# A gated mixer projected token-major: v's input as the stationary operand, its weights moving, in two passes over the weights

## The chip, the cores and the metric

One core of a Trainium2 chip runs the kernel. The metric is device time in microseconds (us), the median of several executions of one program. One more execution was taken with the profiler on; the rows below come from that one.

## The reference, cut to what matters

One layer of a hybrid decoder works on 2048 prompt tokens and on 8 samples of one token each, D_MODEL = 1024, everything in float32:

```
h = rms_norm(x) * (1 + scale(c)) + shift(c)                 # adaLN
p = h @ w_in        # columns: q k v (3*512) | z 512 | beta alpha | u 512 | vb 512
# head group A: gated DeltaNet, 4 heads of 128, chunks of 64, with a running state
# head group B: spatial gating
vn = rms_norm_per_head(gelu(vb)) * w                        # per token and head, over 128
v2 = w_sgu[h] (128x128, lower triangular) applied over the tokens of a 128-chunk + b
mixB = gelu(u) * v2
x1 = x + gate * ([mixA, mixB] @ w_out)
y  = x1 + gate2 * ConvFFN(adaLN(x1))
# each sample also updates its own states S (4 heads x 128 x 128):  S <- eg*S + k v^T
```

Two facts matter here. The sgu of head group B normalizes vb over the 128 channels of a head, and then mixes over tokens. And each sample has a state of 128x512 numbers that is read, updated and written back.

## The kernel before, in words

**Precision.** A float32 operand is split into a high and a low part (`split`: ACT copies the high part, L100, and DVE subtracts for the low one, L97). A product is three matmuls: high by high, high weights by low input, low weights by high input (`gemm_steps`, L113 to L115). Ordinarily the weights are the stationary operand (128x128) and the input hh, hl, channel-major, is the moving one, so that results stand with channels on the partitions and tokens along the free axis.

**Stages.** The mixer runs over four segments of 512 prompt tokens. Segment 0 also carries the samples' 8 columns: 520 columns, in blocks of 2x260. A segment does q, k and v of the delta group (`qkv_tile`, with the 16 squarings and solves of the chunks between), then the sgu's four heads (`sgu`, and `sgu_post` one head behind), then the z tiles woven with the delta chain (`scan`), then the out projection (`out_proj`, with the next segment's first stage between its tiles). The FFN follows, in three column blocks.

**Weights.** A block of weights is 128x512 in two parts, 512 KB (`wblock`). In segment 0 it comes raw through SP's queue (`wslab`, L147, tile wr, 128x1024 and so two blocks), is split on ACT and DVE, used, and stored in DRAM, also through SP's queue (L160, `kept_*`). From segment 1 on POOL's queue reads the stored 512 KB back (L156, `w<-kept_w_in`). Raw and split tiles share one ring of six (tag "w").

**PSUM.** Products use three banks (tag g), transposes and small results two (tag t), the chain's results two (tag c).

**Order.** A scheduler arranges each engine's instructions within what the tiles allow. Each engine, and each engine's DMA queue, runs its instructions strictly in the order that results: an instruction that waits holds back everything behind it. On SP that means that a store that waits for its data holds the loads behind it.

**The sgu before.** `sgu(h)` projects v (act_tile(20 + h)) and u (act_tile(16 + h)) with channels on the partitions. `sgu_post` transposes v back to token rows on PE (four 128x128 transposes, L653), sums squares on ACT (L424), takes root and reciprocal (L657, L658), scales on DVE (L660, four), applies the 128x128 token mixing on PE (L664), and multiplies by u on POOL.

**The delta chain's inversion.** `solve_merge` writes the solved blocks to DRAM (`td<-sv`, L508) and reads them back in another layout (`lt<-td`, L511) into one of three tiles with tag lt. DVE rearranges them, and PE multiplies (L525).

**The samples' states.** `smp_state` runs between the out projection's tiles of segment 0. For each of eight samples a 256 KB state is loaded (L759, tile cv), DVE makes a masked key (L847, km), PE makes the outer products (L849), DVE combines (L851, four), and SP stores the state (L853). The states go through tiles with tag cv. There are four, and the masked values vm hold one.

Of the kernel before, what the change touches and what calls it, by code (L numbers as in the profile page):

```python
# [45 lines left out]
def trunk(ctx, tc, A, O):  # L46
# [98 lines left out]
    def wslab(src):  # L145
        raw = wp.tile([128, 1024], F32, tag="w", name="wr", bufs=6)
        nc.sync.dma_start(out=raw, in_=src)  # L147
        return raw
# [152 lines left out]
    def cv_slabs():  # L301
        while True:
            yield cv()[:, 0:512]
# [333 lines left out]
    def act_tile(*a):  # L637
        run(act_steps(*a))

    def sgu(h, hx, W, extra):  # L640
        uv = uvt()
        act_tile(20 + h, hx, W, AF.Gelu_apprx_tanh, uv[:, 0, 0:SEG], gvs[:, h, :])
        next(extra, None)
        act_tile(16 + h, hx, W, AF.Gelu_apprx_tanh, uv[:, 1, 0:SEG], us[:, h, :])
        next(extra, None)
        return uv

    def sgu_post(h, uv, W, mix):
        off = W - SEG
        v, u = uv[:, 0, 0:SEG], uv[:, 1, 0:SEG]  # L650
        tp = pst()
        for t in range(4):
            PE.transpose(tp[:, t * 128:(t + 1) * 128], v[:, t * 128:(t + 1) * 128], ident)  # L653
        ss = small((128, 4), "sgs")
        for t in range(4):
            square_sum(tp[:, t * 128:(t + 1) * 128], ss[:, t:t + 1], "v")
        S_.activation(out=ss, in_=ss, func=AF.Sqrt, scale=1.0 / 128, bias=epst[:, 0:1])  # L657
        V.reciprocal(out=ss, in_=ss)  # L658
        for t in range(4):
            V.tensor_scalar(out=v[:, t * 128:(t + 1) * 128], in0=tp[:, t * 128:(t + 1) * 128],  # L660
                            scalar1=ss[:, t:t + 1], scalar2=None, op0=ALU.mult)
        ps = pst()
        for t in range(4):
            PE.matmul(ps[:, t * 128:(t + 1) * 128], v[:, t * 128:(t + 1) * 128], wsT[:, h, :], start=True, stop=True)  # L664
# [161 lines left out]
    def smp_state(sk, vn, eg):  # L826
# [13 lines left out]
        vm = cv()[0:32, 0:512].rearrange("p (h v) -> p h v", h=4)  # L840
# [3 lines left out]
        for b in range(NS):  # L844
            s0 = load_state(b, cv()[:, 0:512])
# [341 lines left out]
    for s in range(NSEG):  # L1187
# [34 lines left out]
        extra = mod_half(4, cv_slabs()) if s == 0 else iter(())  # L1222
        for hd in range(4):
            uv = sgu(hd, h, W, extra)
            if hd:
                sgu_post(hd - 1, pend, W, mix)
            else:
                v_head(3, vf[3], Z)
                solve_merge(Z)
# [6 lines left out]
        sgu_post(3, pend, W, mix)  # L1236
# [120 lines left out]
def _layout(i):  # L1357
# [19 lines left out]
        "w_in": tiles(cols), "w_ba": w_in[:, 2048:2056].reshape(8, 128, 8).transpose(1, 0, 2),  # L1377
# [43 lines left out]
```

## Time and profile before

| | us |
|---|---|
| median of 3 runs | 2552.92 (2552.12 to 2553.29) |
| profiled execution | 2546.75 |
| span of its records | 2545.0 |
| PE busy, share of the span | 2422.3, 95% |
| DVE busy | 1701.6, 67% |
| ACT busy | 1040.6, 41% |
| POOL busy | 631.6, 25% |

The profiled execution lies 6.2 us under the median of the runs without a profile, and 1.75 us of it lie outside the span. A change that is worked out from rows moves the span, and is then added to the median. A busy time counts the time in which an instruction of the engine runs. A busy PE can still run at half its clock, which a row of the windows shows as a granted clock of 0.50.

### The profile page before, as it was taken

Reading aid. Unit: us, or ns where it says so; the run is one execution under the profiler, and the core shown is the slowest. Engines: PE = TensorE matmul, PEld = TensorE weight load, DVE = VectorE, ACT = ScalarE, POOL = GpSimd, SP = SyncE. Lnnn points to the kernel's source line nnn. Section 1 sums busy time; section 2 is a strip of 40 time slices with the busy share of each in tenths; the row PEclk is TensorE's granted clock in tenths of the full one; section 3 lists DMA queues with packets and bytes.
Section 4 is the critical chain, followed back from the end, with each engine's and each line's share of the span. In section 5 each row is a group of like instructions: output and inputs, shape, how many; then the busy total and the mean of one; then the engine's idle time right before and its main releaser. Section 6 shows DMA issues by size and latency. Waiting matters only on the chain.

```text
span 2545.0 us, 41928 instructions
## 1 busy us (share of the span) xinstructions
PE 2422.3 (95%) x15770; PEld 2241.5 (88%) x15770; DVE 1701.6 (67%) x3603; ACT 1040.6 (41%) x2137; POOL 631.6 (25%) x897
## 2 busy tenths in 40 slices
PE   7889989999999999989999998899999898999997
PEld 4788967888888878889999998899999898999997
DVE  4676667454735563799999998665556685665565
ACT  5756635465445634454444444322222242211213
POOL 0110003211311221311111115433333353333333
PEclk9999989999999999999999999999999999999998
DMA  9775777566746664898777778877777668776773
GB/s 370 243 255 173 255 230 252 158 194 195 203 129 211 213 172 135 288 330 310 289 296 288 296 284 294 265 244 231 230 225 228 218 211 265 232 230 219 229 233 118
DMA packets 224058, 600.86 MB, mean 236 GB/s; under 512 B 39344, under 2 KB 67696, under 8 KB 223344
## 3 DMA queue, kind: packets, MB, share of 16 engines
q0 software_dynamic: 84672, 308.32, 38.7%
q1 hardware_dynamic: 129824, 280.24, 31.1%
q10 hardware_dynamic: 9360, 9.63, 1.2%
q8 instruction: 125, 2.05, 0.3%
q14 instruction: 77, 0.63, 0.1%
HBM read 430.39 MB, written 167.70 MB: 235 GB/s over the span
## 4 chain that ended last, share of the span: by engine, by line
PE 67%; DVE 16%; DMA 9%; ACT 4%; issue 3%; SPq 1%; POOL 0%; ACTq 0%; DVEq 0%; POOLq 0%
PE u L114 8%; PE u L113 8%; PE u L115 8%; PE g L113 6%; PE g L114 6%; PE d L113 6%; PE g L115 6%; PE d L115 6%; PE d L114 6%; DVE acc L1014 2%; DVE wb L97 1%; DVE TP L500 1%; DVE cv L370 1%; DVE sv L502 1%; DVE w L97 1%
## 5 line engine op out<-in xcount | busy, mean ns | idle before, releaser
L113 PE MATMUL d<-midh,w 128*128 128x344 f32 (+1 forms) x1032 | 329.4, 324 | 36.3 <-DVE xa L1078 24.4
L113 PE MATMUL g<-hh,w 128*128 128x512 f32 (+1 forms) x960 | 347.6, 362 | 2.1 <-ACT cv L366 2.1
L1014 DVE SCALAR_TENSOR_TENSOR acc<-raw,vec,acc 128x680 f32<-128x680 f32 (+1 forms) x264 | 299.6, 1137 | 66.4 <-ACT acc L1007 63.6
L114 PE MATMUL g<-hl,w 128*128 128x512 f32 (+1 forms) x960 | 341.7, 356 | 0.0
L113 PE MATMUL u<-T,wb 128*128 128x344 f32 (+1 forms) x1056 | 338.2, 321 | 3.3 <-DVE mc L1020 2.4
L115 PE MATMUL g<-hh,w 128*128 128x512 f32 (+1 forms) x960 | 340.1, 355 | 0.0
L114 PE MATMUL u<-T,wb 128*128 128x344 f32 (+1 forms) x1056 | 337.6, 320 | 1.4 <-DVE T L97 1.4
L115 PE MATMUL u<-T,wb 128*128 128x344 f32 (+1 forms) x1056 | 335.8, 319 | 0.9 <-DVE wb L97 0.9
L114 PE MATMUL d<-midl,w 128*128 128x344 f32 (+1 forms) x1032 | 330.7, 321 | 0.0
L1078 DVE SCALAR_TENSOR_TENSOR xa<-d,mod,xa 128x344 f32<-128x344 f32 (+2 forms) x376 | 210.8, 569 | 173.7 <-PE d L115 154.6
L115 PE MATMUL d<-midh,w 128*128 128x344 f32 (+1 forms) x1032 | 325.6, 322 | 0.6 <-DVE w L97 0.6
L1007 ACT ACTIVATE acc<-raw,vec 128x680 f32<-128x680 f32 (+1 forms) x132 | 126.0, 956 | 406.2 <-DVE raw L1002 401.0
L113 PE MATMUL u<-B,wb 128*128 128x344 f32 (+1 forms) x792 | 253.5, 321 | 9.0 <-ACT B L100 6.9
L114 PE MATMUL u<-B,wb 128*128 128x344 f32 (+1 forms) x792 | 254.0, 321 | 1.3 <-DVE B L97 1.3
L115 PE MATMUL u<-B,wb 128*128 128x344 f32 (+1 forms) x792 | 252.6, 319 | 0.0
L113 PEld LDWEIGHTS d<-midh,w 128*128 128x128 f32 x1032 | 195.1, 190 | 41.9 <-DVE xa L1078 16.0
L113 PEld LDWEIGHTS g<-hh,w 128*128 128x128 f32 x960 | 183.4, 191 | 33.1 <-issue 4.5
L115 PEld LDWEIGHTS g<-hh,w 128*128 128x128 f32 x960 | 182.7, 190 | 27.1 <-issue 2.1
L114 PEld LDWEIGHTS g<-hl,w 128*128 128x128 f32 x960 | 183.7, 191 | 25.6 <-issue 0.8
L113 PEld LDWEIGHTS u<-T,wb 128*128 128x128 f32 x1056 | 199.1, 189 | 4.6 <-DVE mc L1020 2.7
L114 PEld LDWEIGHTS u<-T,wb 128*128 128x128 f32 x1056 | 199.0, 188 | 2.4 <-DVE T L97 2.3
L115 PEld LDWEIGHTS u<-T,wb 128*128 128x128 f32 x1056 | 198.9, 188 | 1.3 <-DVE wb L97 1.2
(388 smaller groups left out, 5032.0 us busy)
## 6 DMA issues: line engine op xcount, KB each, us to landing
wb<-kept_w_up_T POOLq DMA_DIRECT2D x176, 512.0 KB, 4.9
w<-kept_w_in POOLq DMA_DIRECT2D x144, 512.0 KB, 3.9
wb<-kept_w_up_B POOLq DMA_DIRECT2D x132, 512.0 KB, 5.0
kept_w_up_T<-wb SPq DMA_DIRECT2D x88, 512.0 KB, 4.5
w<-kept_w_down POOLq DMA_DIRECT2D x88, 512.0 KB, 4.9
kept_w_up_B<-wb SPq DMA_DIRECT2D x66, 512.0 KB, 4.0
kept_w_in<-w SPq DMA_DIRECT2D x48, 512.0 KB, 4.7
w<-kept_w_out POOLq DMA_DIRECT2D x48, 512.0 KB, 4.4
```

What stands on the lines that cost most here:

```text
L97: (eng or V).tensor_tensor(out=out, in0=a, in1=hi.bitcast(F32), op=ALU.subtract)
L113: PE.matmul(ps[:, :n], wh, mh[:, c0:c0 + n], start=k == ks[0], stop=False)
L114: PE.matmul(ps[:, :n], wh, ml[:, c0:c0 + n], start=False, stop=False)
L115: PE.matmul(ps[:, :n], wl, mh[:, c0:c0 + n], start=False, stop=k == ks[-1])
L370: V.scalar_tensor_tensor(out=acc, in0=cr[:, j:j + SEG], scalar=vc("cqkv", ft * 4 + j), in1=acc, op0=ALU.mult, op1=ALU.add)
L500: V.tensor_tensor(out=tmp, in0=NB[:, j, j + 1:32].unsqueeze(2).to_broadcast([64, r, w]), in1=TB[:, j:j + 1, 0:w].to_broadcast([64, r, w]), ...
L502: V.tensor_tensor(out=TB[:, j + 1:32, 0:w], in0=TB[:, j + 1:32, 0:w], in1=tmp, op=ALU.subtract)
L1007: S_.activation(out=acc[:, off:W], in_=raw[:, 2:2 + m], func=AF.Identity, scale=vc("cffn", ft * 3 + 2), bias=vc("cffb", ft))
L1014: V.scalar_tensor_tensor(out=acc[:, off:W], in0=raw[:, j:j + m], scalar=vc("cffn", ft * 3 + j), in1=acc[:, off:W], op0=ALU.mult, op1=ALU.add)
L1078: V.scalar_tensor_tensor(out=xa[ft][:, b0 + o:b0 + n], in0=ps[:, o:n], scalar=mod[:, 40 + ft, 0:1], in1=xa[ft][:, b0 + o:b0 + n], op0=ALU. ...
```

## The change

v of the sgu is no longer projected tile by tile with its weights stationary. A new function, `vb_tokens`, does it ahead of the sgu's loop: 128 tokens of the input (hh, hl) are the stationary operand and the weights (128x512) are moving, so that the result has tokens on the partitions and all four heads' channels along the free axis. Two PSUM banks hold two groups of 128 tokens, and so the eight blocks of weights are gone through twice, once for each half of the segment. The weights have their own array `w_vb` (8 blocks of 128x512). In segment 0 the first half loads them raw (256 KB), splits and stores them, and the second half reads them back; in the other segments both halves read them back. In segment 0 the second half also does the 8 sample columns as a third group, whose result is transposed back. Scaling takes one DVE instruction for a group of tokens and all heads. `sgu_post` keeps only the token mixing. The four v results take the four cv tiles. So the slabs of the modulation's fifth part now go through sv tiles, and the samples' states and vm through the three lt tiles.

```diff
-    def wslab(src):
-        raw = wp.tile([128, 1024], F32, tag="w", name="wr", bufs=6)
+    def wslab(src, n=1024):
+        raw = wp.tile([128, 1024], F32, tag="w", name="wr", bufs=6)[:, 0:n]
         nc.sync.dma_start(out=raw, in_=src)
         return raw
...
-    def cv_slabs():
+    def sv_slabs():
         while True:
-            yield cv()[:, 0:512]
+            t = sv()
+            yield t[:, 0:512]
+            yield t[:, 512:1024]
...
+    def vb_tokens(hx, W, s):
+
+        off = W - SEG
+        out = []
+        for half in range(2):
+            ts = (2 * half, 2 * half + 1)
+            ps = [psg() for _ in ts]
+            if off and half:
+                ps.append(psg())
+            for k in range(KT):
+                key, w = ("w_vb", k), wpt()
+                raw = None
+                if key not in kept:
+                    raw = wslab(A["w_vb"][k], 512)
+                wblock(key, w, raw)
+                hh, hl = hx[k]
+                for j, p in enumerate(ps):
+                    c = slice(off + 128 * ts[j], off + 128 * ts[j] + 128) if j < 2 else slice(0, NS)
+                    o = p[0:c.stop - c.start, :]
+                    PE.matmul(o, hh[:, c], w[:, 0], start=k == 0, stop=False)
+                    PE.matmul(o, hh[:, c], w[:, 1], start=False, stop=False)
+                    PE.matmul(o, hl[:, c], w[:, 0], start=False, stop=k == KT - 1)
+            for j, p in enumerate(ps):
+                if j == 2:
+                    m = nm()
+                    V.memset(m[:, 0:512], 0.0)
+                    S_.activation(out=m[0:NS, 0:512], in_=p[0:NS, :], func=AF.Gelu_apprx_tanh)
+                    tp = pst()
+                    for h in range(4):
+                        PE.transpose(tp[:, h * 128:(h + 1) * 128], m[:, h * 128:(h + 1) * 128], ident)
+                    V.tensor_copy(out=gvs, in_=tp.rearrange("p (h c) -> p h c", h=4)[:, :, 0:NS])
+                    continue
+                v = cv()[:, 0:512]
+                S_.activation(out=v, in_=p, func=AF.Gelu_apprx_tanh)
+                ss = small((128, 4), "sgs", 4)
+                for h in range(4):
+                    square_sum(v[:, h * 128:(h + 1) * 128], ss[:, h:h + 1], "v")
+                S_.activation(out=ss, in_=ss, func=AF.Sqrt, scale=1.0 / 128, bias=epst[:, 0:1])
+                V.reciprocal(out=ss, in_=ss)
+                v4_ = v.rearrange("p (h i) -> p h i", h=4)
+                V.tensor_tensor(out=v4_, in0=v4_, in1=ss.unsqueeze(2).to_broadcast([128, 4, 128]), op=ALU.mult)
+                out.append(v4_)
+        return out
+
     def sgu(h, hx, W, extra):
         uv = uvt()
-        act_tile(20 + h, hx, W, AF.Gelu_apprx_tanh, uv[:, 0, 0:SEG], gvs[:, h, :])
-        next(extra, None)
         act_tile(16 + h, hx, W, AF.Gelu_apprx_tanh, uv[:, 1, 0:SEG], us[:, h, :])
...
-        tp = pst()
-        for t in range(4):
-            PE.transpose(tp[:, t * 128:(t + 1) * 128], v[:, t * 128:(t + 1) * 128], ident)
-        ss = small((128, 4), "sgs")
-        for t in range(4):
-            square_sum(tp[:, t * 128:(t + 1) * 128], ss[:, t:t + 1], "v")
-        S_.activation(out=ss, in_=ss, func=AF.Sqrt, scale=1.0 / 128, bias=epst[:, 0:1])
-        V.reciprocal(out=ss, in_=ss)
-        for t in range(4):
-            V.tensor_scalar(out=v[:, t * 128:(t + 1) * 128], in0=tp[:, t * 128:(t + 1) * 128],
-                            scalar1=ss[:, t:t + 1], scalar2=None, op0=ALU.mult)
         ps = pst()
         for t in range(4):
-            PE.matmul(ps[:, t * 128:(t + 1) * 128], v[:, t * 128:(t + 1) * 128], wsT[:, h, :], start=True, stop=True)
+            PE.matmul(ps[:, t * 128:(t + 1) * 128], vt[t][:, h, :], wsT[:, h, :], start=True, stop=True)
...
-        vm = cv()[0:32, 0:512].rearrange("p (h v) -> p h v", h=4)
+        vm = lt()[0:32, 0:512].rearrange("p (h v) -> p h v", h=4)
...
-            s0 = load_state(b, cv()[:, 0:512])
+            s0 = load_state(b, lt())
...
-        extra = mod_half(4, cv_slabs()) if s == 0 else iter(())
+        vt = vb_tokens(h, W, s)
+        extra = mod_half(4, sv_slabs()) if s == 0 else iter(())
```

Three places of the order that the scheduler makes are shown. The first is SP's queue in segment 0, where the sgu's first weights come in (a number behind `kept_...` is the tile's own). Before, at the end of the third v tile of the delta group:

```order
L160 DMA kept_w_in_0_1826<-w 128x1024
L147 DMA wr<-in_w_in 128x1024
L160 DMA kept_w_in_1_1831<-w 128x1024
L160 DMA kept_w_in_0_1943<-w 128x1024
L147 DMA wr<-in_w_in 128x1024
L160 DMA kept_w_in_1_1948<-w 128x1024
```

And in the changed program, from the same store on:

```order
L160 DMA kept_w_in_0_1826<-w 128x1024
L147 DMA wr<-in_w_vb 128x512
L160 DMA kept_w_in_1_1831<-w 128x1024
L147 DMA wr<-in_w_vb 128x512
L160 DMA kept_w_vb_1944<-w 128x1024
L147 DMA wr<-in_w_vb 128x512
L160 DMA kept_w_vb_1957<-w 128x1024
L147 DMA wr<-in_w_vb 128x512
L160 DMA kept_w_vb_1970<-w 128x1024
```

One raw slab used to give two blocks, and one load stood for two stores. Now each block has a load of its own, and the load of a slice stands behind the store of the slice two before it.

The second is PE in segment 0's out projection, at the samples' states (`smp_state`). Before, the first two states' products stood together, 18 products followed, and then the other six states' in one piece, here with the products on both sides of it:

```order
L114 MATMUL g<-hl,w 128x512
L115 MATMUL g<-hh,w 128x512
L849 MATMUL t<-cv,sv 128x512 x6
L113 MATMUL g<-hh,w 128x512
L114 MATMUL g<-hl,w 128x512
```

In the changed program, from the first state's product to beyond the second:

```order
L883 MATMUL t<-lt,sv 128x512
L115 MATMUL g<-hh,w 128x512
L113 MATMUL g<-hh,w 128x512
L883 MATMUL t<-lt,sv 128x512
L114 MATMUL g<-hl,w 128x512
L115 MATMUL g<-hh,w 128x512
```

The six that stood together are now spread: 2 products stand between the first and the second, then 14 (with one group of L455), 11, 19, 10, 21 and 26 between each and the next. Of these 103, 40 have 512 columns and 63, the later ones, 260 (the out projection's).

The third is ACT in segment 1 where `vb_tokens` goes from its first half to its second. Before, at the first sgu tile:

```order
L481 ACTIVATE ve<-t,rt 128x128 x4
L635 ACT_TABLE_LOAD
L635 ACTIVATE uv<-g 128x512 x2
L481 ACTIVATE ve<-t,rt 128x128 x4
L635 ACTIVATE uv<-g 128x512 x2
```

In the changed program:

```order
L376 ACTIVATE cv<-cv 128x512
L483 ACTIVATE ve<-t,rt 128x128 x8
L675 ACT_TABLE_LOAD
L675 ACTIVATE cv<-g 128x512 x2
L426 ACTIVATE jk,sgs<-cv 128x128 x4
L679 ACT_TABLE_LOAD
```

The gelu that empties the first half's two banks stands behind two groups of evictions of the delta group's v (L483, which was L481; eight instructions), where one group of four stood ahead of it.

## Rows read from the trace of the kernel before

**Rows 1.** Page, first section: busy time, share and instructions of each engine.

```profile
PE 2422.3 (95%) x15770; PEld 2241.5 (88%) x15770; DVE 1701.6 (67%) x3603; ACT 1040.6 (41%) x2137; POOL 631.6 (25%) x897
```

**Rows 2.** Windows: us, busy of PE, PEld, DVE, ACT, POOL, PEclk, DMA share, GB/s.

```profile
270.00:280.00 10.00, 10.00 (x86) 10.00 (x85) 7.70 (x33) 8.66 (x20) 0.00 (x0) 1.00 1.04 399
340.00:350.00 10.00, 6.66 (x8) 1.69 (x7) 4.50 (x17) 1.15 (x2) 0.00 (x0) 0.50 0.81 267
450.00:460.00 10.00, 10.00 (x47) 8.10 (x46) 6.58 (x22) 5.18 (x12) 2.07 (x4) 1.00 0.64 200
```

**Rows 3.** Timeline of PE in segment 1: start us, us, instruction.

```profile
441.01 0.39 PE L113 MATMUL g<-hh,w 128*128 128x512 f32 x1
...
441.94 0.60 PE L479 MATMUL t<-ident,cv 128*128 128x128 f32 x4
442.29 0.48 PE L114 MATMUL g<-hl,w 128*128 128x512 f32 x1
```

**Rows 4.** Timeline of PE in segment 0.

```profile
157.06 0.28 PE L113 MATMUL g<-hh,w 128*128 128x260 f32 x1
157.18 0.28 PE L114 MATMUL g<-hl,w 128*128 128x260 f32 x1
```

**Rows 5.** Timeline of all engines in segment 0: one raw slab, its split, its store.

```profile
150.30 0.38 SPq L147 DMA_DIRECT2D wr<-in_w_in  x1
...
154.96 0.63 ACT L100 ACTIVATE w<-wr 128x512 fp32r<-128x512 f32 x1 [2.48 <-DMA wr<-in_w_in]
...
155.63 0.69 DVE L97 TENSOR_TENSOR w<-wr,w 128x512 fp32r<-128x512 f32 x1 [0.23 <-ACT w L100]
...
156.35 0.32 SPq L160 DMA_DIRECT2D kept_w_in<-w  x1
```

**Rows 6.** DMA issues: tensors, engine, count, KB each, median us to landing.

```profile
w<-kept_w_in POOLq DMA_DIRECT2D x144, 512.0 KB, 3.9
...
S<-in_w_down SPq DMA_DIRECT2D x44, 256.0 KB, 4.0
...
cv<-in_st_delta SPq DMA_DIRECT2D x8, 256.0 KB, 4.6
...
out_nd_s<-cv SPq DMA_DIRECT2D x8, 256.0 KB, 3.1
```

**Rows 7.** Chain that ended last, in order of time: start us, us, what.

```profile
174.50 6.93 DMA td<-sv
...
181.50 8.07 DMA lt<-td
...
695.13 2.90 DMA td<-sv
...
698.93 6.77 DMA lt<-td
```

**Rows 8.** Waits of PE: in total us, times, longest.

```profile
PE c L525 <- DMA lt<-td: 5.2, 3, 1.9
```

**Rows 9.** Timeline of ACT in segment 1.

```profile
451.35 1.13 ACT L481 ACTIVATE ve<-t,rt 128x128 f32<-128x128 f32 x4
452.50 1.28 ACT L635 ACT_TABLE_LOAD   x1
453.79 0.60 ACT L635 ACTIVATE uv<-g 128x512 f32<-128x512 f32 x1
```

**Rows 10.** Timeline of PE in segment 0's out projection, at the samples' states.

```profile
329.54 1.98 PE L849 MATMUL t<-cv,sv 32*128 32x512 f32 x4
...
335.83 1.98 PE L849 MATMUL t<-cv,sv 32*128 32x512 f32 x4
...
352.92 0.79 PE L113 MATMUL g<-hh,w 128*128 128x512 f32 x1 [2.13 <-ACT cv L366]
...
356.41 0.39 PE L115 MATMUL g<-hh,w 128*128 128x512 f32 x1
```

**Rows 11.** Groups by line, each shape apart, DVE: busy, mean ns, idle before.

```profile
L851 DVE SCALAR_TENSOR_TENSOR cv<-cv,sv,t 128x128 f32<-128x128 f32 x32 | 8.9, 340 | 5.3 <-DMA cv<-in_st_delta 5.3
```

More of the change, by code (lines that the diff above doesn't have):

```diff
@@ L640, in sgu, with sgu_post @@
     def sgu(h, hx, W, extra):
         uv = uvt()
-        act_tile(20 + h, hx, W, AF.Gelu_apprx_tanh, uv[:, 0, 0:SEG], gvs[:, h, :])
-        next(extra, None)
         act_tile(16 + h, hx, W, AF.Gelu_apprx_tanh, uv[:, 1, 0:SEG], us[:, h, :])
         next(extra, None)
+        next(extra, None)
         return uv
-    def sgu_post(h, uv, W, mix):
+    def sgu_post(h, uv, W, mix, vt):
         off = W - SEG
         v, u = uv[:, 0, 0:SEG], uv[:, 1, 0:SEG]
-        tp = pst()
-        for t in range(4):
-            PE.transpose(tp[:, t * 128:(t + 1) * 128], v[:, t * 128:(t + 1) * 128], ident)
-        ss = small((128, 4), "sgs")
-        for t in range(4):
-            square_sum(tp[:, t * 128:(t + 1) * 128], ss[:, t:t + 1], "v")
-        S_.activation(out=ss, in_=ss, func=AF.Sqrt, scale=1.0 / 128, bias=epst[:, 0:1])
-        V.reciprocal(out=ss, in_=ss)
-        for t in range(4):
-            V.tensor_scalar(out=v[:, t * 128:(t + 1) * 128], in0=tp[:, t * 128:(t + 1) * 128],
-                            scalar1=ss[:, t:t + 1], scalar2=None, op0=ALU.mult)
@@ L1225, in trunk @@
             if hd:
-                sgu_post(hd - 1, pend, W, mix)
+                sgu_post(hd - 1, pend, W, mix, vt)
             else:
@@ L1235, in trunk @@
             smp_mix(mix, 4, smp_sgu())
-        sgu_post(3, pend, W, mix)
+        sgu_post(3, pend, W, mix, vt)
         for _ in extra:
@@ L1376, in _layout @@
         "xT": x.T, "cT": c.T.reshape(8, 128, 9).transpose(1, 0, 2), "w_mod": f("w_mod")[0],
-        "w_in": tiles(cols), "w_ba": w_in[:, 2048:2056].reshape(8, 128, 8).transpose(1, 0, 2),
+        "w_in": tiles(cols[:, :2560]), "w_vb": cols[:, 2560:].reshape(8, 128, 512), "w_ba": w_in[:, 2048:2056].reshape(8, 128, 8).transpose(1, 0, 2),
         "w_out": tiles(f("w_out")[0]), "w_up": tiles(f("w_up")[0]),
```

## The prediction

> **What bounds the kernel now.** I read the busy times first. PE is busy for 95% of the span [rows 1], so the time changes by what is added to or taken from PE's instructions, and by what makes PE wait. Then I read the windows: in most stretches PE has no idle time, at the full clock (450 to 460 us, DMA share 0.64), and the same holds where the DMA engines are saturated at 399 GB/s (270 to 280 us). A stretch of the out projection of segment 0 differs: PE is busy for two thirds of it and its granted clock is 0.50 (340 to 350 us) [rows 2]. The timelines, transfers and waits then price the three places that the change touches: the v projection, its start in segment 0, and the samples' states. About 0.2% (5.1 us) is what a measurement of this kernel can tell from no change.
>
> **Samples' states.** The third pair of L849 begins at 335.83 us, and the next product at 352.92. In these 17.1 us PE does only six states' products; two of them take 1.98 us, so six take 5.9 and 11.2 us are lost [rows 10]. The nine products from 352.92 to 356.41 take 3.49 us, against 9 x 0.233 = 2.1 at the full clock (0.233 is the spacing of 512 columns: four products from 441.01 to 441.94 [rows 3]), which is 1.4 more. The loss is 12.6 us.
>
> Afterwards the states' products stand one by one among 103 others. What may hold them is the tiles, two for the states where there were three. A tile's round is a store of 3.1 us and a load of 4.6 [rows 6], four combinations of 0.34 us on DVE [rows 11] and issue, some 9 to 10 us. A state's product doesn't read the tile; it needs a PSUM bank, and so the combination two states before. PE's own work from the first product to the last is 40 x 0.233 + 63 x 0.12 (the spacing of 260 columns [rows 4]) + 8 x 0.99 = 24.8 us. The eighth product needs the sixth combination, two rounds and a little behind the second product, some 20 us; PE's own work brings it there after 23.8. So it should hardly wait, and I leave 2.3 us for waits on the way. Gain: 12.6 - 2.3 = **10.3 us**. At best it is 12.6. At worst DVE, which runs in order, waits for each of the last three rounds and keeps evictions behind it: DVE waited 5.3 us for loads before [rows 11], and three rounds at 3 us leave 3.6.
>
> **Segment 0.** PE's work first. Four v tiles are 192 products of 260 columns, 192 x 0.12 = 23.0 us. Now there are 96 with 512 columns and 24 more for the samples, 120 x 0.233 = 28.0. Four transposes cost PE 0.36 us (441.94 to 442.29 [rows 3], and a slower start of the product behind); 12 of 16 go, which is 1.1. Net 28.0 - 23.0 - 1.1 = +3.9.
>
> The first half uses a slice of 256 KB up in six products, 1.39 us, and waits for its raw load. The load of a slice stands on SP behind the store of the slice two before. So two slices take one round: the issue (0.35), the landing (4.0 to 4.6, the rows of 256 KB loads [rows 6]), and the split (154.96 to 156.35, 1.40) [rows 5]. That is 5.8 to 6.4 us, 6.1 in the middle, where PE needs 2.8. Three rounds follow the second slice, which I place at 157 us, since the split in [rows 5] ends at 156.3: the first half ends at 157 + 18.3 + 1.4 = 176.7. PE alone, beginning at 156.7 just ahead of [rows 4], would end at 156.7 + 8 x 1.39 = 167.8. That is +8.9. With the fastest 256 KB row (3.1, a store) a round is 4.85 and it is +5.1. If one round meets dense transfers and its landing takes 4.0 us more, as the td trip did in segment 0 (6.93 against 2.90 [rows 7]), it is +12.9.
>
> At the change of halves the second half's first bank must be emptied by a gelu: I take +1.0 as in the other segments (below). The wait of PE for lt, 1.7 us on average [rows 8], goes, since PE comes some 10 us later. The gate products and transposes that the order puts between the slices lie in the waits, about 0.4 for one group of transposes. Sum for segment 0: 3.9 + 8.9 + 1.0 - 1.7 - 0.4 = **+11.7** (7.9 to 15.6).
>
> The granted clock bears on this. At 340 to 350 us PE worked in pieces of a few us with waits between, and the clock was 0.50 [rows 2]; the first half will look like this. Six products at that clock take 6 x 0.39 = 2.3 us [rows 10], under the round's 3.05 a slice, so only the last slice and the start of the second half get longer. The Trainium skill, "TensorE: Matmul & The Clock Gate", section "HAM oscillation — how this bites in real kernels", speaks against such a loop: where a K-tile's work is shorter than the wait for its next slice, every K-tile starts cold, and it advises to restructure. The trace agrees as far as the 0.50 goes. By that rule the sum would be about 2.3 us higher, 0.9 for the last slice and 1.4 as in the run-up above.
>
> **Segments 1 to 3.** 96 products of 512 columns stay 96. The 16 transposes go: 4 x 0.36 = -1.44 each, -4.3 together. The weights are read twice: 512 KB per 1.39 us is 377 GB/s in the pass, against 200 measured in the sgu before and 399 where the engines are saturated [rows 2]. The ring's six tiles turn over in 8.3 us, a landing takes 3.9 [rows 6] and its use 1.39, so PE isn't starved as long as a landing stays under 6.9.
>
> At the change of halves three banks are turned: the gelu comes behind four evictions (1.13), a table load (1.28) and itself takes 0.60 [rows 9]. In part these run before the half ends. I take a third of the 3.0, +1.0 a segment (0 to 3.0), so +3.0.
>
> The td and lt trip took 10.6 us in segment 2 (695.13 to 705.70), and 15.1 in segment 0, whose loads and stores are the denser [rows 7]. It now falls into the pass. 377 lies 0.89 of the way from 200 to 399, which makes it 3.9 us longer, and half of that if its last part meets the end of the pass; I take 3.0. PE's first product with lt stands 42 to 54 v products behind the last transposes of the delta group, instead of 48, and has the bank wait ahead of it: it comes 0.25 us earlier in segment 1 and 2.7 later in segments 2 and 3. In segment 1 PE didn't wait for lt (three waits for four segments [rows 8]), so I give it 0.5 of slack: 3.0 + 0.25 - 0.5 = 2.75, and 0.3 for each of the other two. Together +3.3 (-3.4 to +8). Sum for the three: -4.3 + 3.0 + 3.3 = **+2.0**.
>
> **At nothing.** DVE loses 64 scalings and gets 16 larger ones, ACT's squares stay, POOL issues 8 more loads a segment. None of the three is near its limit, DVE at 67% [rows 1] being closest, and PE's products cover them; without that cover DVE's 16 would cost 11 us at the 0.69 of a DVE pass over 128x512 [rows 5]. The slabs in sv tiles are loaded through the same queue as before.
>
> **The sum.** -10.3 + 11.7 + 2.0 = +3.4 us. The profiled execution (2546.75, its span 2545.0) would become 2550.2. The median of the runs shown, 2552.92, is 6.2 higher, and becomes **2556.3**.
>
> **Rivals.**
>
> - A, the forecast: +3.4 us, 2551 to 2561 with its own terms. Chance 0.40.
> - B, faster: the pass leaves the td and lt trip alone (10.6 us as in segment 2) and the banks are empty in time. The place is the sgu of segments 1 to 3. For it: PE has 1.39 us a block and POOL runs ahead. Against it: 377 GB/s is near the 399 of the saturated stretch. Segments 1 to 3 then give -4.3, and the waits for lt of segments 2 and 3, 1.7 each, go as well because PE comes later: -7.7. Total -10.3 + 11.7 - 7.7 = -6.3, so 2546.6. It decides if lt is late by less than 1 us. Chance 0.23.
> - C, slower: the pass saturates the engines. The trip takes 15.1 in all segments, 4.5 more: PE waits 4.25 longer in segment 1 and 1.8 in each of the others, and PE's wait brings the clock down, 1.4 a segment as at 352.92 to 356.41. Segments 1 to 3: -4.3 + 3.0 + 7.85 + 4.2 = +10.75; total +12.1, 2565.1. It decides from landings of some 7 us on. Chance 0.22.
> - D, slower too: two tiles are too few for the states, and DVE's waits pass on to PE. The gain is 3.6: total -3.6 + 11.7 + 2.0 = +10.1, 2563.0. For it: one SP queue holds stores, loads and the out projection's raw weights. Against it: the products don't wait for the tiles themselves. Chance 0.15.
>
> **How the numbers follow.** The range takes in B with some more gain (a first half at its lower bound) and C with one more late round: 2542 to 2568. Faster by over 0.2% are most of B and the lowest of A, 0.25; slower are C, most of D and the upper end of A, 0.39; the rest is 0.36.
>
> **What would show it.** Right: in segment 0 PE waits for w in the first half about every 3 us, for some 9 us in all, with a fall of the granted clock; the states' stretch has a clock of 1.00 and no gap over 2 us; segments 1 to 3 run the pass without waits for w, one wait of about 1 us at the change of halves, and up to 3 us for lt. Wrong: the first half runs without waits; the states' products wait for sv or t; or w comes late in segments 1 to 3, where each 1 us per block would cost up to 16 us a segment.

## The result, and the profile after

The changed kernel takes 2566.01 us (median of 6 runs, 2558.32 to 2568.47), and the kernel before, with more runs on the same chip, 2552.13 (6 runs, 2549.46 to 2553.29). The ratio is 1.0053, with a 95% interval of 1.0039 to 1.0067: 13.5 us slower, by 10.0 to 17.1. The forecast was 2556.3, within 2542 to 2568, with "slower" as the likeliest sign. The time lies beside rival C (2565.1), and above the 2551 to 2561 that rival A, the forecast, had for itself.

The profiled execution after has a span of 2559.6 us, 14.6 more than before. PE is busy for the same share of it; of the first section of the page (busy, share, instructions of each engine; before [rows 1]):

```profile
PE 2432.6 (95%) x15638; PEld 2239.9 (88%) x15638; DVE 1693.9 (66%) x3557; ACT 1039.8 (41%) x2127; POOL 648.9 (25%) x929
```

To find where the time goes I compared the moments at which PE does the same instruction in the two traces. PE is 0.8 us late when it finishes the chunk products of q and k in segment 0 (135 us), and 8.9 late at the end of its delta chain (266 us). It is 2.4 early by the norm sums behind the out projection (396 us): the states gave back 10.7 us. Segment 1's sgu and chain make it 4.2 late (533 us), segment 2's 12.7 (772 us), segment 3's 13.3 (1015 us). In the FFN one more microsecond is added. So segment 0 costs 8.1 us, the states gain 10.7, and segments 1 to 3 cost 15.7, for which I had +2.0.

What PE waits for says most (waits of PE: us in total, times, longest; before [rows 8]):

```profile
PE c L527 <- DMA lt<-td: 19.8, 4, 6.6
...
PE g L661 <- DMA w<-kept_w_vb: 2.6, 3, 1.5
PE g L661 <- ACT w L100: 2.2, 2, 1.8
```

PE waits 19.8 us for the inversion's trip through DRAM, where it waited 5.2. The trip itself, in the chain that ended last (start us, us, what; before [rows 7]):

```profile
455.32 5.09 DMA td<-sv
...
460.43 8.75 DMA lt<-td
...
699.32 4.27 DMA td<-sv
...
705.10 14.30 DMA lt<-td
...
947.16 4.88 DMA td<-sv
...
952.06 11.16 DMA lt<-td
```

From the first issue to the last end in a chain these are 13.9 us in segment 1, 20.1 in segment 2 and 16.1 in segment 3; segment 2 took 10.6 before. (The chain ends with the read that something waited for, which isn't the same of the four reads each time; a table below has the same read throughout.) The timeline of PE shows what the wait does (start us, us, instruction, in brackets the idle time before it):

```profile
463.29 0.39 PE L663 MATMUL g<-w,hl 128*128 128x512 f32 x1
469.22 0.31 PE L527 MATMUL c<-lt,nz 32*32 32x32 f32 x2 [5.54 <-DMA lt<-td]
...
471.76 0.63 PE L661 MATMUL g<-w,hh 128*128 128x512 f32 x1
472.19 0.63 PE L662 MATMUL g<-w,hh 128*128 128x512 f32 x1
```

In segment 1 the first product with lt stands inside the pass over v. PE stands still for 5.5 us there, although the weights of the next v products have landed (by 464.0 us), and the products behind it come 0.43 us apart and not 0.233: the granted clock has fallen to its lower level, 1.2 GHz. In segments 2 and 3 the product stands just behind the last one of the pass, and PE waits 5.1 and 6.6 us. The windows say the same (us, busy of PE, PEld, DVE, ACT, POOL, PEclk, DMA share, GB/s):

```profile
442.00:452.00 10.00, 10.00 (x47) 8.09 (x46) 9.55 (x25) 3.62 (x9) 3.67 (x7) 1.00 0.84 260
452.00:462.00 10.00, 9.86 (x46) 7.77 (x45) 3.93 (x15) 8.62 (x27) 3.23 (x7) 1.00 1.04 339
462.00:472.00 10.00, 4.46 (x19) 3.48 (x18) 1.52 (x3) 1.06 (x1) 1.06 (x2) 0.73 1.15 262
```

In segment 1 the pass itself runs without a gap up to 462 us. In segment 2 PE waits 1.8 us in all for w, in segment 3 not at all, and at no change of halves for a bank. So the doubled reading of the weights hardly starves PE; what it delays is another transfer.

The states' stretch is as forecast. PE has one wait from 326 to 396 us, and not at a state's product; the clock is 1.00 where it was 0.50 [rows 2]:

```profile
PE t L440 <- DVE smp L718: 0.6, 1, 0.6
```

```profile
338.00:348.00 10.00, 10.00 (x38) 5.85 (x37) 9.82 (x31) 7.56 (x11) 0.00 (x0) 1.00 0.62 200
348.00:358.00 10.00, 10.00 (x48) 6.99 (x47) 7.64 (x24) 7.68 (x13) 0.00 (x0) 1.00 0.81 258
```

In segment 0 the first half of the v pass takes 18.7 us (155.4 to 174.1) where PE alone needs 11.2:

```profile
155.00:165.00 10.00, 10.00 (x55) 6.49 (x54) 9.01 (x23) 5.04 (x13) 0.00 (x0) 1.00 0.91 304
165.00:175.00 10.00, 6.97 (x22) 3.74 (x21) 5.11 (x16) 4.04 (x6) 1.82 (x4) 0.90 0.92 299
175.00:185.00 10.00, 10.00 (x35) 6.26 (x35) 1.74 (x4) 5.04 (x20) 2.61 (x5) 0.76 1.05 314
```

Of the 7.5 us between the two, PE stands still for 3.0 (0.4, 1.8 and 0.8). Gate products and one group of transposes, which the order puts between the slices, take 2.0, and the rest is slower starts behind a pause and the clock, which is 0.50 from 173 to 180 us. SP's queue in the middle of the half (timeline of SP: start us, us, instruction):

```profile
159.94 0.38 SPq L160 DMA_DIRECT2D kept_w_vb<-w  x1
160.42 0.38 SPq L147 DMA_DIRECT2D wr<-in_w_vb  x1
161.69 0.33 SPq L160 DMA_DIRECT2D kept_w_vb<-w  x1
162.11 0.59 SPq L147 DMA_DIRECT2D wr<-in_w_vb  x1
166.32 0.33 SPq L160 DMA_DIRECT2D kept_w_vb<-w  x1
166.75 0.37 SPq L147 DMA_DIRECT2D wr<-in_w_vb  x1
```

Each load goes out 0.4 to 0.5 us behind the store of the slice two before, and has no wait of its own.

### The profile page after: what moved, and what is told of

Read it like the earlier page. It is cut to its first block, busy times and chain, and to the rows that moved or that the text cites. A ratio compares the mean times of both kernels' runs of the same rounds, so it can differ in the third digit from the quotient of the medians.

```text
span 2559.6 us, 41690 instructions
## 1 busy us (share of the span) xinstructions
PE 2432.6 (95%) x15638; PEld 2239.9 (88%) x15638; DVE 1693.9 (66%) x3557; ACT 1039.8 (41%) x2127; POOL 648.9 (25%) x929
## 4 chain that ended last, share of the span: by engine, by line
PE 66%; DVE 17%; DMA 10%; issue 3%; ACT 3%; SPq 1%; POOL 0%; ACTq 0%; DVEq 0%; POOLq 0%
PE u L113 8%; PE u L114 8%; PE u L115 8%; PE g L113 6%; PE d L113 6%; PE g L114 6%; PE g L115 6%; PE d L115 5%; PE d L114 5%; DVE acc L1048 2%; DVE cv L372 2%; DVE wb L97 1%; DVE TP L502 1%; DVE sv L504 1%; DMA lt<-td 1%
## 5 line engine op out<-in xcount | busy, mean ns | idle before, releaser
L113 PE MATMUL g<-hh,w 128*128 128x512 f32 (+1 forms) x800 | 290.6, 363 | 0.0
L114 PE MATMUL g<-hl,w 128*128 128x512 f32 (+1 forms) x800 | 285.5, 357 | 0.0
L115 PE MATMUL g<-hh,w 128*128 128x512 f32 (+1 forms) x800 | 284.5, 356 | 0.0
L113 PEld LDWEIGHTS d<-midh,w 128*128 128x128 f32 x1032 | 196.2, 191 | 39.8 <-issue 14.5
L114 PEld LDWEIGHTS d<-midl,w 128*128 128x128 f32 x1032 | 197.3, 191 | 0.0
L115 PEld LDWEIGHTS d<-midh,w 128*128 128x128 f32 x1032 | 195.7, 191 | 1.3 <-DVE w L97 1.3
L1061 POOL TENSOR_TENSOR mc<-mc 128x344 f32<-128x344 f32 (+1 forms) x66 | 70.5, 1069 | 418.1 <-ACT mc L1060 351.4
```

Source lines behind the costliest of these rows:

```text
L113: PE.matmul(ps[:, :n], wh, mh[:, c0:c0 + n], start=k == ks[0], stop=False)
L114: PE.matmul(ps[:, :n], wh, ml[:, c0:c0 + n], start=False, stop=False)
L115: PE.matmul(ps[:, :n], wl, mh[:, c0:c0 + n], start=False, stop=k == ks[-1])
L1061: G.tensor_tensor(out=u, in0=u, in1=m7, op=ALU.add)
```

## Experiments

My theory after the result: in segments 1 to 3 the second reading of the weights slows the td and lt trip, PE meets the late lt inside the pass, and loses the wait and then half its clock for a while. The rivals: PE only comes earlier to its first product with lt, whatever the traffic; or the pass itself is the cost. For segment 0 the theory was SP's order, for the states the number of tiles.

Kernels that ran together share a chip and the runs of before on it: 2550.01 for the first four, 2552.41 for the next four, 2550.4 for the next three, 2551.29 for the last. Runs of one kernel spread by some 10 us, more than those of before on the first chip did; the intervals take account of it. Differences between kernels below are those of their medians. By the ratios, which leave the chip out, the 28 us of the one pass are 25, the 22 of the later lt 21, and the 10 of its second reading 8.

**The states alone.** The kernel before with two lines of the change:

```diff
-        vm = cv()[0:32, 0:512].rearrange("p (h v) -> p h v", h=4)
+        vm = lt()[0:32, 0:512].rearrange("p (h v) -> p h v", h=4)
...
-            s0 = load_state(b, cv()[:, 0:512])
+            s0 = load_state(b, lt())
```

> The kernel before with only the samples' states and their masked values moved from the cv tiles to the lt tiles; v is projected as before. If the states' stretch is worth what the two traces show between the start of the out projection and the next segment's norm sums (about 11 us), this gives 2541 us (2538 to 2545), with no loss elsewhere. The rival, that the gain of this stretch in the changed kernel came from the new v path (another arrangement around it), expects 2549 to 2553.

Measured: 2545.46 us (7 runs), ratio 0.9968 (0.9956 to 0.9980), 8.2 us less. The same moments of PE show 9.6 us gained between 312 and 396 us. The rest of the mixer gained 4 more, and the FFN lost 11. So the gain is the states' own, and it doesn't need the new v path.

**The v path alone.** The changed kernel with these two lines put back.

```diff
-        vm = lt()[0:32, 0:512].rearrange("p (h v) -> p h v", h=4)
+        vm = cv()[0:32, 0:512].rearrange("p (h v) -> p h v", h=4)
...
-            s0 = load_state(b, lt())
+            s0 = load_state(b, cv()[:, 0:512])
```

> The changed kernel with the states and their masked values back in the cv tiles. If the two parts add up, the token-major v alone costs what the whole change costs plus the states' gain: 2566 + 11 = 2577 us (2572 to 2581). If the parts interact (the new v path spreads the states by itself) it stays near 2566.

Measured: 2582.5 us (4 runs), ratio 1.0126 (1.0101 to 1.0151), 32 us more than before, and outside what I expected. Between the two moments around the states PE loses 12.2 us against the changed kernel, which is the states' part and adds up. Another 10 us of the profile's 22 lie in the FFN, 7 of them in its first column block, which differs by 5 us between two executions of the kernel before (below). So the stretch is settled, and the sum of the two parts, 32 - 8 = 24 for the 13.5 measured together, is not.

**The traffic alone, on the kernel before.**

```diff
         raw = None if (name, i, 0) in kept else wslab(A[name][i])
+        if raw is None and name == "w_in" and i in (16, 17, 20, 21):
+            ws = []
+            for j in range(2):
+                G.dma_start(out=wpt(), in_=kept[name, i, j])
+                ws += wblock((name, i, j), wpt())
+            return ws
```

> The kernel before, computing v as before, but in segments 1 to 3 each of the eight blocks of the first two v and u tiles of the sgu is loaded a second time into a ring tile that nothing reads: the traffic of the two passes alone. Theory (the doubled reading slows the td and lt trip): the trip grows from 10 to 12 us to 14 to 20, PE waits for lt some 4 to 8 us a segment, 2562 to 2572 us in all. Rival (PE only reaches its first product with lt earlier after the delta group's solve): the trip stays under 13 us and the time within 4 us of before.

Measured: 2562.37 us (10 runs, 2551.55 to 2570.89), ratio 1.0048 (1.0029 to 1.0067): 12 us slower with v computed as before. The profiled execution was the fastest of the ten (2551.55), so its trace shows less than the median. In it the single transfers of the trip took 6.9 us in the middle, against 5.5 before, and PE waited 4.7 us for lt, no more than before. At 12.4 to 15.2 us to its last landing the trip is longer than before (9.6 to 11.8), but mostly short of the 14 to 20 that I expected, and the waits of 4 to 8 us a segment aren't there. Segments 1 to 3 take 4.9 us more than before in this trace. The traffic costs time; where the other runs' share lies, no trace shows.

**One pass in segments 1 to 3.** Four banks, the fourth that of the modulation, which is idle there; each block is read once.

```diff
-        for half in range(2):
-            ts = (2 * half, 2 * half + 1)
-            ps = [psg() for _ in ts]
+        for half, ts in enumerate([(0, 1), (2, 3)] if off else [(0, 1, 2, 3)]):
+            ps = [psg() for _ in ts[:3]]
+            if not off:
+                ps.append(pm.tile([128, 512], F32, tag="m", name="m"))
...
-                    c = slice(off + 128 * ts[j], off + 128 * ts[j] + 128) if j < 2 else slice(0, NS)
+                    c = slice(off + 128 * ts[j], off + 128 * ts[j] + 128) if j < len(ts) else slice(0, NS)
...
-                if j == 2:
+                if j == len(ts):
```

> The changed kernel, but in segments 1 to 3 all four groups of tokens go in one pass over the weights, the fourth in the PSUM bank of the modulation, so that each block is read once. Theory (doubled reading): the trip falls back to 10 to 12 us, PE's waits for lt to 1 to 3 us a segment; 15 us less than the changed kernel, give or take 4, so 2548 to 2556 us, with a new wait of about 2 us a segment at the end of the pass, when all banks are emptied at once. Rival (PE comes earlier to its first product with lt, whatever the traffic): the waits stay at 4 us and more, 2560 to 2566 us.

Measured: 2538.2 us (5 runs), ratio 0.9956 (0.9940 to 0.9971), 28 us less than the changed kernel and below before. PE's whole wait for lt, and the trip of segment 3 (chain):

```profile
PE c L527 <- DMA lt<-td: 0.5, 1, 0.5
```

```profile
924.75 4.70 DMA td<-sv
...
930.43 6.18 DMA lt<-td
```

To the landing of the last read the trip is 12.1 us there, against 18.2 with two passes. PE comes to its first product with lt 8.6 to 11.1 us after the issue of the store, as in the changed kernel (8.4 to 12.2), and now lt is there. So the rival, that PE only comes earlier, falls. The wait of 2 us that I expected at the end of the pass isn't there either. The gain is larger than I had expected: PE's waits for lt fall by 19 us and not by 11 to 17, and I had left out the clock, which is 1.00 in all three of these stretches.

**One pass, and the traffic of two.**

```diff
+                if not off:
+                    G.dma_start(out=wpt(), in_=kept[key])
```

> The version with one pass in segments 1 to 3, with each of its eight blocks loaded a second time into a ring tile that nothing reads: the traffic of the two passes, and PE's order of the one pass. Theory (doubled reading slows the td and lt trip): the trip goes from 10 to 12 us back to 15 to 20, PE's waits for lt from 0.5 us to 10 to 18 in all, the time from 2538 to 2548 to 2560 us. Rival (PE's order in the two passes, not the traffic): trip under 13 us, time within 4 us of 2538.

Measured: 2548.41 us (10 runs), ratio 0.9986 (0.9973 to 0.9999): 10 us more than with one reading. Segment 3's trip in the chain (td stored from 930.04, lt there at 946.96) is back at 16.9 us (17.1 to the last landing):

```profile
930.04 8.02 DMA td<-sv
...
938.98 7.98 DMA lt<-td
```

PE waits for lt only 2.1 us, though. The scheduler had put the first products with lt later (behind 471 and 710 us in segments 1 and 2, when lt had landed), and what PE waits for is w (5.0 us in all). The lower end of the expected time is met, the expected waits for lt (10 to 18 us) are not. So the traffic makes the trip long; how much that costs depends on where PE's order puts the first product with lt.

**Both passes, the first product with lt later.** In segments 1 to 3 lt also waits for the first u tile.

```diff
+        if after is not None: V.scalar_tensor_tensor(out=Tn[:, 0:1], in0=after, scalar=0.0, in1=Tn[:, 0:1], op0=ALU.mult, op1=ALU.add)
         V.transpose(out=tr, in_=Tn)
...
-                solve_merge(Z)
+                solve_merge(Z, uv[:, 1, 511:512] if s else None)
```

> The changed kernel with both passes, but in segments 1 to 3 the first products with lt also wait for the first u tile (one more DVE instruction of one column, which adds zero times a value of u). In the order PE then has the pass and two u tiles (47 more products, 11 us) ahead of them. Theory (the doubled reading makes the trip long, and PE meets it inside the pass, stands still and loses its clock): the trip stays at 15 to 20 us but PE doesn't wait for lt, the clock stays at 1.00, and the time falls by the 18 us of waits and half clock less what the later chain costs: 2547 to 2555 us. Rival (the pass itself costs, by late weights or banks): 2560 us and more.

Measured: 2543.68 us (10 runs), ratio 0.9971 (0.9953 to 0.9988), 22 us less than the changed kernel, with all its traffic. The windows of the pass's end in segment 1, and the trip of segment 3 in the chain:

```profile
454.00:464.00 10.00, 10.00 (x47) 7.98 (x46) 3.14 (x12) 8.00 (x25) 3.71 (x7) 1.00 1.05 342
464.00:474.00 10.00, 10.00 (x49) 8.23 (x48) 1.66 (x4) 6.81 (x20) 2.65 (x5) 1.00 1.35 314
```

```profile
930.05 4.42 DMA td<-sv
...
936.64 13.92 DMA lt<-td
```

The trip takes 20.5 us, no shorter than in the changed kernel; that it is longer because PE goes on and with it the loads is likely but not shown. PE's longest wait for lt is 0.1 us, its clock is 1.00 through all three segments, and the later chain costs nothing that shows: segments 1 to 3, which cost 15.7 us in the changed kernel, are 12.9 shorter than before in this trace, which is that of the fastest run. With the trip as long as ever and the wait gone, the loss is gone: the cost was where PE stood when lt was late, and the clock behind it. The rival, that the pass itself costs, falls.

The three segments side by side, worked out from the traces. All numbers are us from the issue of the store of td, for segments 1, 2 and 3. Where PE comes before the first read has landed, the difference is its wait:

| kernel | first read of lt landed | PE at its first product with lt | last read landed |
|---|---|---|---|
| before | 6.5, 8.2, 7.7 | 10.2, 8.5, 8.5 | 9.6, 11.2, 11.8 |
| changed | 13.9, 17.3, 16.1 | 8.4, 12.2, 9.5 | 16.6, 20.3, 18.2 |
| before, doubled reading | 11.3, 10.9, 12.0 | 11.2, 12.5, 11.4 | 12.9, 12.4, 15.2 |
| one pass | 7.2, 7.3, 8.6 | 10.8, 8.6, 11.1 | 10.2, 10.1, 12.1 |
| one pass, traffic of two | 12.7, 12.0, 14.5 | 18.4, 19.8, 14.6 | 14.0, 14.2, 17.1 |
| both passes, lt later | 16.6, 15.2, 15.9 | 23.5, 21.6, 20.7 | 22.6, 19.8, 20.5 |

Of these, only the changed kernel has PE there well ahead of the first read. The doubled reading alone makes the read late, and PE's order decides whether it costs a wait.

**Segment 0: raw slices on another queue.** The eight raw loads through POOL's queue, so that none stands behind a store.

```diff
-        nc.sync.dma_start(out=raw, in_=src)
+        (nc.sync if n == 1024 else G).dma_start(out=raw, in_=src)
```

> The changed kernel with the eight raw slices of segment 0 loaded through POOL's queue and not SP's, so that no load stands behind a store of a split slice. If that order sets the first half's pace (my step: two slices a round of 6.1 us), the first half falls from 18 us to 13 to 15 and the time by 3 to 6 us, to 2560 to 2563. If it is the landing or the split that sets the pace, the first half stays at 17 to 18 us and the time at 2566.

Measured: 2579.16 us (4 runs), ratio 1.0097 (1.0071 to 1.0123). The first half took 20.0 us (156.8 to 176.8), no less. So lifting SP's order alone doesn't raise the pace. Now the raw loads wait on POOL's queue for a tile of the ring (waits of POOL, 145 to 175 us):

```profile
POOL wr L147 <- DVE TP L502: 10.5, 3, 5.0
POOL wr L147 <- PE g L663: 8.0, 2, 4.1
```

The second half took 29.7 us, against 20.3 in the changed kernel: POOL's queue, in order too, now holds the re-reads behind raw loads that wait, and PE waits 5.4 us for lt there.

**Segment 0: raw slices in other tiles.**

```diff
-                    raw = wslab(A["w_vb"][k], 512)
+                    raw = lt(); nc.sync.dma_start(out=raw, in_=A["w_vb"][k])
```

> The changed kernel with the eight raw slices of segment 0 in the three lt tiles and not in the ring of six that they share with the split blocks. If the ring sets the first half's pace (a split block holds its place until its store has landed, and raw slices stand behind it), the first half falls from 18 us to 13 to 15 and the time by 3 to 5, to 2561 to 2563. If it stays at 17 to 18 us, the landing and the split in turn set it, or SP's order, as I had predicted.

Measured: the first half takes 13.0 us (155.5 to 168.5), and PE has no gap in it:

```profile
155.00:165.00 10.00, 10.00 (x50) 7.95 (x50) 8.91 (x24) 6.25 (x15) 2.06 (x4) 1.00 0.90 293
165.00:175.00 10.00, 10.00 (x43) 6.01 (x40) 7.97 (x26) 6.89 (x22) 2.38 (x5) 1.00 1.08 388
```

At the end of segment 0's delta chain PE is 1.6 us behind before, and not 8.9. But this edit lifts two things at once. The raw slices no longer share the ring, and with three tiles of their own the fourth load stands behind the store of the first slice, so of the slice three before and not two:

```profile
147.32 0.32 SPq L160 DMA_DIRECT2D kept_w_vb<-w  x1
147.69 1.55 SPq L655 DMA_DIRECT2D lt<-in_w_vb  x1
```

So what set the pace is how far ahead the raw slices may be loaded. In the changed kernel SP's order holds a load until the store of the slice two before, and with that order lifted the ring holds it; no run parts the two any further. The median, however, is 2566.35 (10 runs, 2555.26 to 2569.34; ratio 1.0051, 1.0034 to 1.0068), as slow as the changed kernel. The stage is faster in the profiled run, which is one of the two fastest of the ten; the median isn't, and no trace shows one of the slower runs.

**One pass everywhere, the modulation's bank in segment 0 too.** In segment 0 the fourth group takes the modulation's bank and the samples one of the transposes'.

```diff
-        for half, ts in enumerate([(0, 1), (2, 3)] if off else [(0, 1, 2, 3)]):
+        for half, ts in enumerate([(0, 1, 2, 3)]):
-            ps = [psg() for _ in ts[:3]]
-            if not off:
-                ps.append(pm.tile([128, 512], F32, tag="m", name="m"))
-            if off and half:
-                ps.append(psg())
+            ps = [psg() for _ in ts[:3]] + [pm.tile([128, 512], F32, tag="m", name="m")]
+            if off:
+                ps.append(pst())
```

> As the version with one pass in segments 1 to 3, and segment 0 in one pass too: four groups in three banks and the modulation's, the samples in one of the transposes' banks. A slice then feeds 15 products, 3.5 us, about the pace of its raw loads, so the first half's wait of 7 us and the slow clock behind it should mostly go: 4 to 8 us less than 2538, 2530 to 2534. If the split on ACT and DVE or the queue sets a slower pace than 3.5 us a slice, or the banks are missed elsewhere, it stays within 3 us of 2538.

Measured: 2546.15 us (10 runs), ratio 0.9974 (0.9959 to 0.9990), 12 us and more above what I expected. Segment 0's pass takes 28.1 us (155.8 to 183.9), all of it PE's work. But the gate products of the modulation, which used to lie in the pass, now wait for their bank (PE's waits from 140 to 300 us):

```profile
PE m L286 <- ACT cv L674: 5.3, 1, 5.3
```

and the clock behind it is 0.50 from 200 to 210 us. At the end of the delta chain PE is 13.1 us behind before, more than with two passes. In segment 0 that bank was in use.

**One pass everywhere, the fourth group in a bank of the transposes, the samples in one of the chain's.** Against the version before it:

```diff
-            ps = [psg() for _ in ts[:3]] + [pm.tile([128, 512], F32, tag="m", name="m")]
+            ps = [psg() for _ in ts[:3]] + [pst() if off else pm.tile([128, 512], F32, tag="m", name="m")]
             if off:
-                ps.append(pst())
+                ps.append(psc())
```

> One pass in all segments; in segment 0 the fourth group takes a bank of the transposes and the samples one of the chain's, so that the modulation keeps its own bank. The version with the modulation's bank lost 5.3 us of wait and some 5 us of half clock to it in segment 0. Without that segment 0 should end 8 to 12 us earlier than there (its mixer then 2 to 5 us behind before instead of 15): 2530 to 2537 us. If the delta chain misses its bank instead, 2540 us and more.

Measured: 2538.79 us (6 runs, 2529.44 to 2544.25), ratio 0.9954 (0.9932 to 0.9975). The pass takes 28.1 us and PE is 4.9 us behind at the end of segment 0's chain, which is about the samples' 24 products (5.6 us). The profile was that of the fastest run; by the median it is no faster than with two passes in segment 0.

**One pass in segments 1 to 3, raw slices in lt.** The version with one pass there, with one line more:

```diff
-                    raw = wslab(A["w_vb"][k], 512)
+                    raw = lt(); nc.sync.dma_start(out=raw, in_=A["w_vb"][k])
```

> The version with one pass in segments 1 to 3, and the raw slices of segment 0 in the lt tiles. In the profile of the changed kernel with raw slices in lt the mixer of segment 0 ended 7 us earlier, but the median of its runs didn't fall. If that gain is real and was hidden by the spread that the two passes bring into segments 1 to 3, this version is 5 to 8 us faster than 2538, 2530 to 2533. If the stage's gain is given back later (the FFN's first column block), it stays at 2536 to 2540.

Measured: 2536.23 us (6 runs, 2530.82 to 2543.95), ratio 0.9936 (0.9916 to 0.9956), 15 us below before on its chip. The expected 2530 to 2533 is missed; the interval overlaps that of the version without it. In its trace PE goes from 2.6 us behind before to 5.8 over segment 0's second part, from 135 to 266 us, where the version without it goes from 0.7 ahead to 6.8 behind: so 4.3 us less, of the 6.7 that raw slices in lt gave in the changed kernel. It has the lowest median here and is faster than before and the changed kernel, but not told apart from the other versions with one pass.

**Before, a second profile.**

> The kernel before, unchanged, for a second profile of the same program: how much its stages differ from one execution to the next. The mixer should agree within 2 us; the FFN's first column block, which took 522 us in the first profile of before and 526 to 533 in those of four other kernels, may differ by up to 8 us if that is a matter of the execution, and stays at 522 if it follows from the kernels.

Measured: 2552.81 us. The mixer of the second profile differs by up to 3.8 us on the way (segment 2) and by 0.0 at its end. The FFN's first column block, taken between the norm sums ahead of it and behind it, takes 527 us and not 522. Here DVE is nearly as busy as PE (480 of 520 us), PE catches up with it, and waits of up to some 3 us come or don't. So the 526 to 533 us of the other kernels are in part a matter of the execution, and single profiles can't be compared to better than 5 us in their sums, and to some 4 us in the mixer's stages.

## Why the prediction was right, and where it was not

The sign was right and the range held the time, but only because the range took in rival C: the forecast's own terms gave 2551 to 2561. The sum was 10 us short. Segments 1 to 3 were 13.7 short, and segment 0, 3.6 too high, hid a part of it.

- **Samples' states, -10.3.** Measured -10.7 in the changed kernel, -9.6 alone. The argument (a product needs a bank and not the tile, so two tiles are enough) held: PE has no wait there. Rival D is out.
- **Segment 0, +11.7.** Measured +8.1. The first half took 18.7 us for the predicted 20.0, and the step "The load of a slice stands on SP behind the store of the slice two before" is what the trace of the changed kernel shows: from store to store, two slices take 5.7 to 6.5 us from the third slice on, for the predicted 6.1. It isn't the only hold, though. With loads freed of the stores the ring of six kept the same pace, and raw slices in three tiles of their own took 5.7 us off. What the step had wrong is PE's share: not some 9 us of waits, but 3.0, since other products fill the pauses.
- **The clock in the first half.** I took the piecewise work to run at 0.50. The rows show 1.00 from 155 to 165 us, and 0.50 only from 173 to 180 us; PE had stood still for 0.4 and 1.8 us in the 8 us before it fell. The Trainium skill, "TensorE: Matmul & The Clock Gate", section "HAM oscillation — how this bites in real kernels", has every K-tile start cold where its work is shorter than the wait for the next slice. The trace has one such wait, 1.8 us before the last slice, beside 1.39 us of work, and even that slice began at the full clock. The long waits for lt in segments 1 to 3, after which the spacing is 0.43 us, are where such a fall does cost.
- **Segments 1 to 3, +2.0.** Measured +15.7: this is the step that failed, "377 lies 0.89 of the way from 200 to 399, which makes it 3.9 us longer ... I take 3.0" (0.89 of the 4.5 us between the two trips is 4.0, a slip of no weight). The trip of segment 2 became 9.5 us longer (20.1 against 10.6), longer than the 15.1 that I had as the upper bound from segment 0. PE's waits for lt came to 19.7 us in the three segments, against 3.4, and to this the clock must be added, which the forecast left out: its mean in the windows of the three mixers' second parts (432 to 537.6, 676 to 785.4 and 924 to 1028.5 us) was 0.97, 0.95 and 0.97, against 1.00, 0.98 and 0.97 before. That is some 7 us of clock (3.2 + 5.5 + 3.1 against 0 + 2.0 + 3.1), part of it while PE waits anyway. With the transposes' -4.3, which nothing contradicts, 16.3 + 7 - 4.3 gives 19, of which 15.7 shows.
- **The change of halves, +3.0,** was nothing: PE has no wait for a gelu in the second parts of segments 1 to 3. Its waits there are those for lt, and 1.8 us for w in segment 2, where the forecast had none.
- **Rival C** had the mechanism, the place and the clock (+10.75 for these segments, 2565.1 in all), at a chance of 0.22. That its sum lies within 1 us of the result is partly luck: it was 5 us short for these segments and kept the 3.6 too many of segment 0. I gave it too little because I compared GB/s. The trip is not a stream of bytes. Its reads are runs of 128 B (2048 packets in the trace of segment 1, 27 ns each in the mean, beside the loads' packets of 4096 B at 189 ns), and with PE's order of the one pass a second reading beside it lengthened it by 4 to 5 us. The Trainium skill, "DMA: Bandwidth & Descriptors", section "Queues, rings and completion order", says that each engine goes round its queues packet by packet; that would make a transfer of many small packets wait at each turn. No run here shows the turns, but the order of the trips agrees (segment 3, to the last landing: 12.1 us with one reading, 17.1 and 18.2 with two, 20.5 with two and a PE that goes on).

What stays open: why the changed kernel's median doesn't fall when segment 0 gets 7 us faster, what part of the 12 us in the kernel before with doubled reading lies in the mixer, since its profile was of the fastest run, and which of the ring and SP's order would hold segment 0's first half without the other.

## What to carry to other kernels

A second reading of weights that PE's own pace can bear is not free: ask which small, late transfer shares the engines with it, and where PE's order meets that transfer. The wait costs the stall and the slower clock behind it; put the first product that needs it behind independent work, or read once (here a spare PSUM bank was enough). And count how many raw slices may be under way at once, by the tiles and by the queue's order: with two ahead the first half took 18.7 us, with three tiles of their own 13.0.

## What the runs showed of the hardware

The windows' DMA share goes well over 1 while the bytes fall: 1.35 at 314 GB/s with the lt trip under way (464 to 474 us, both passes and lt later), where the saturated stretch before had 1.04 at 399 GB/s [rows 2]. GB/s, by which I had priced the trip, orders these two stretches the other way round than the engines' busy share does.
